# Hybrid attention and mLSTM layer on one core: two projections by seven products of quarter size in place of eight

## The chip, the core and the metric

The kernel runs on one core of a Trainium2 chip. The metric is the device time of one execution in microseconds; three runs of the kernel before have a median of 896.19 us (895.63 to 897.06). Engines are called PE (TensorE), DVE (VectorE), ACT (ScalarE), POOL (GpSimd) and SP (SyncE, which issues the transfers).

## What is computed

One decoder layer with two token mixers on the same normalised input of 512 tokens and 1024 channels. Cut to what matters:

```python
xn = rmsnorm(h, norm_in_g)
proj = xn @ w_in                                  # 1024 x 12288
q_a, k_a, v_a, z_a, x_m, z_m, o_m, gates = jnp.split(proj, SPLIT_POINTS, axis=-1)
y_a = (dilated_attention(q_a, k_a, v_a, rel_bias) * silu(z_a)) @ w_pa
y_m = mlstm_branch(x_m, z_m, o_m, ...) @ w_pb     # ends with  h * silu(z_m)
g = sigmoid(gates + gate_b)
g_a, g_m = jnp.split(g, 2, axis=-1)
h = h + (g_a * y_a + g_m * y_m) @ w_out
return rmsnorm(h, norm_out_g)
```

In the mLSTM branch x_m passes a causal convolution and a SiLU, gives q, k and v by small block-diagonal matrices, and each of four heads of 512 channels mixes the tokens with a decay from its input and forget gates; the result is gated with sigmoid(o_m), normalised, added to a skip of x_c, and multiplied with silu(z_m). z_m (2048 columns of w_in) and gates (2048 columns) are the two projections that the change touches.

## The kernel before

All data are float32, and each product is done in three: both factors are split into a high part (fp32r) and a low part, and `mm3` issues high x high, high x low and low x high into one PSUM bank. A projection takes w_in in 96 chunks of 1024 x 128 (on chip 128 x 1024: eight steps of 128 rows of the contraction). `weights` (L420) fetches a chunk on SP into a `raw` tile, and `halves` (L412) splits it: ACT copies it to `whi`, DVE subtracts to `wlo`. `proj_t` (L536) then makes 8 x 3 matmuls of 128 weight columns by 512 tokens into one of two banks of the tag "mm"; six other banks (tag "x") serve scores, transposes and the rest. There are four buffers each of `raw`, `whi` and `wlo`, and 51 "slot" tiles of 516 columns for everything of one token tile.

Stages, in order of the program: the x_m chunks with convolution, folded q/k and the score sums S of each head (`sraw`, four tiles that are kept in SBUF); the gate chain of the mLSTM (gsum, nab, ex, lnu, aa, aT); then for each head `head`(L777): decay weights Wh and Wl, num (60 matmuls), the gated and normalised tho, four z_m chunks with SiLU (`silu2`, L771), the transposes hT, then v and the output gate o_m of the next head (`block_v`, `gate_o`), and the ym projection; then attention (qa, ka, va, za, sa, pT, pv), the 16 gate chunks, ya, out and the last normalisation.

The order is not the program's. A `Recorder` (L101) collects every operation with its dependences, and `issue` (L231) simulates the five engines with a cost for each operation: when an engine is free, it issues the ready operation with the smallest priority for whose new tiles there is room. The priority is the place in the program less `R.ahead` (weights get `AHEAD` = 300, some evacuations of banks `EMPTY` = 300). The engines then run that order as it stands, each in order. All operations are recorded at one place, so the profile gives L333 as the line of every operation; the names of tiles tell them apart.

Of the kernel before, what the change touches and what calls it, by code (L numbers as in the profile page):

```python
# [11 lines left out]
F32 = mybir.dt.float32  # L12
F32R = mybir.dt.float32r
# [4 lines left out]
P = 128  # L18
# [319 lines left out]
def hybrid_layer(ctx, tc, a, out):  # L338
# [43 lines left out]
    def mm3(ps, lh, ll, rh, rl, first, last):  # L382
        PE.matmul(ps, lh, rh, start=first, stop=False)
        PE.matmul(ps, lh, rl, start=False, stop=False)
        PE.matmul(ps, ll, rh, start=False, stop=last)

    def rsqrt(v, n, name):
        y = small(name + "_y", n)
# [39 lines left out]

    ident = const("ident", [P, P], F32)
    pc = const("pc", [P, PC_N], F32)  # L430
    EARLY, UNNORMED, FIRST = 4, 10, 5
    pair = [wide("xt") for _ in range(NK // 2)]
# [5 lines left out]
    def x_split(k):  # L438
        h, l = slot("xh", F32R)[:, :T], slot("xl", F32R)[:, :T]
# [25 lines left out]
    xu = []  # L465
    early_ps = [mm_bank("xm") for _ in range(2)]
    for k in range(NK):
        xu.append(x_split(k))
# [54 lines left out]
        return m  # L523

    R.ahead = 5000
    early_m = [x_m(c, early_ps[c], rb) for c in range(EARLY)]
    R.ahead = 0
    xh, xl = [], []

    def normalise(k):  # L530
        V.tensor_mul(xt[k], xt[k], rb)
        h, l = x_split(k)
        xh.append(h)
        xl.append(l)
# [99 lines left out]
    sxd = dram("sxd", [NMT, P, T])  # L634
    v_of = {}

    def block_v(h):

        b = spread(brow[:, 2], h, "Bv")
        xm = []  # L640
        for c in range(4):
            x_ = slot("xmr")[:, :T]
            SP.dma_start(x_, xmd[4 * h + c])
            xm.append(x_)
        v_of[h] = []
        for s in range(NT):
            ps = sc_bank("v")
            for c in range(4):
                PE.matmul(ps[:, c * P:(c + 1) * P], xm[c][:, s * P:(s + 1) * P], b[:, c * P:(c + 1) * P],
                          start=True, stop=True)  # L650
            v1, v2 = slot("vh", F32R)[:, :514], slot("vl", F32R)[:, :514]
# [4 lines left out]
            v_of[h].append((v1, v2))  # L656

    gps = pv_bank("gates")
    sps = None
    waiting = []  # L660
    sraw = []
    for ct in range(NMT):
        h, c = divmod(ct, 4)
        raw_x = ct < UNNORMED
        ps = None if ct < EARLY else proj_t(CXM + ct, "xm", xu if raw_x else None)
# [21 lines left out]
        A.activation(kf, ps[:, T - P:], AF.Copy)  # L687
        if ct == 0:
            fold_gates()
        waiting.append((ct, m, xc))  # L690
        if c == 3:

            R.together()
            for ct_, m_, xc_ in waiting:
                for i, (w, x) in enumerate(((1, m_[:, 3:259]), (1, m_[:, 259:515]), (0, xc_[:, :256]), (0, xc_[:, 256:]))):
                    PE.matmul(gps[32 * i:32 * i + 32, :256], ust[w][:, ct_, :], x, start=ct_ == 0, stop=ct_ == NMT - 1,
                              tile_position=(0, 32 * i))
            R.apart()
            waiting = []
        for j in range(NT - 1):  # L700
            t0 = j * P
            ss = slice(t0, t0 + P)
            mm3(sps[j][:, :T - t0], kh[:, ss], kl[:, ss], ch[:, t0:], cl[:, t0:], c == 0, c == 3 and j < 2)
        PE.matmul(sps[2][:, 256:384], kf, xc[:, T - P:], start=False, stop=c == 3)
        if c == 3:
            sr = wide("sraw")
            A.activation(sr[:, 0:512], sps[0], AF.Copy)
            A.activation(sr[:, 512:896], sps[1][:, :384], AF.Copy)
            A.activation(sr[:, 896:1280], sps[2][:, :384], AF.Copy)
            sraw.append(sr)  # L710

    def row(name, dt=F32):
        return slot(name, dt)[:4, :T]
# [38 lines left out]
    selr = const("selr", [36, 4, P], F32)  # L752
    SP.dma_start(selr, a["sel"])
    sel = const("sel", [36, 4, P], F32R)
    V.tensor_copy(sel, selr)
# [18 lines left out]
        V.scalar_tensor_tensor(z, z, 1.0, ps, op0=OP.add, op1=OP.mult)  # L774
        return z

    def head(h):  # L777
        ps = sc_bank("Abc")
        PE.matmul(ps, sel[:, h, :], A2, start=True, stop=True)
        Abc = slot("Abc")[:, :T]  # L780
        A.activation(Abc, ps, AF.Copy)
        wh, wl = wide_t("Wh"), wide_t("Wl")
        sr = sraw[h]
        off = (0, 512, 896, 1152)
        for j in range(NT):
# [44 lines left out]
        V.tensor_mul(rs, rs, rr)  # L830
        for t in range(NT):
            V.tensor_scalar(us[t], us[t], mv[:, 2 * t:2 * t + 1], rs[:, t:t + 1], op0=OP.subtract, op1=OP.mult)
        z = [silu2(proj_t(CZM + 4 * h + c, "zm"), "zm") for c in range(4)]
        sx = []
        for c in range(4):
            x_ = slot("sxr")[:, :T]
# [32 lines left out]
    def rel_rows():  # L869
# [5 lines left out]
        G.tensor_copy(ohr, onehot)  # L875
# [17 lines left out]
    def values(p):  # L893
# [90 lines left out]


    ga = []
    for d in range(NK):
        for g in range(2):
            ps = proj_t(CG + NK * g + d, "gate")
            th = slot("thg")[:, :T]  # L990
            A.activation(th, ps, AF.Tanh, scale=0.5, bias=hs[:, 32 + 8 * g + d:33 + 8 * g + d])
            if g == 0:
                ga.append(th)
            else:
                V.scalar_tensor_tensor(ym[d], th, 1.0, ym[d], op0=OP.add, op1=OP.mult)
    go = const("go", [P, D], F32)
# [14 lines left out]
    for d in range(NK):  # L1011
        raw = raw_chunk("raw")
        SP.dma_start(raw, a["w_out"][d * P:(d + 1) * P, :])
        if d < 2:
            wl_ = wide("woh", F32R), wide("wol", F32R)
        elif d < 4:
            wl_ = wide_t("woh"), wide_t("wol")
        else:
            wl_ = None
        pieces = []  # L1020
# [39 lines left out]


NSMALL = 40
NSLOT = 51
NRAW = 4
NHL = 4
AHEAD = 300
EMPTY = 300
NWIDE = 4
NWT = 4


def _bucket(dist):
# [86 lines left out]
```

## Time and profile before

| | |
|---|---|
| median of 3 runs | 896.19 us |
| the profiled execution, its own time | 894.47 us |
| its span in the profile | 892.5 us |
| PE busy, matmuls | 879.0 us, 4340 |
| PE weight loads busy | 723.0 us |
| DVE busy | 573.9 us, 1193 instructions |
| ACT busy | 402.2 us, 750 instructions |
| moved by DMA | 104.64 MB, 117 GB/s on average |

The span is what the profiler sees from the first to the last instruction; the execution's own time is 1.97 us longer. On the scale of the span, the x_m stage ends at 157 us, head 0's om and the gate chain end at 177, the heads at 493, attention at 703, the gate chunks at 797, ya at 841, out at 886. A line of the profile names engine, operation, output and inputs (out<-in), and shapes. A matmul's listed duration contains pipelining, so that matmuls overlap; what one costs is the distance from one start to the next.

### The profile page before, as it was taken

How to read it: one execution, taken by the hardware profiler on the slowest of the kernel's cores; microseconds unless marked ns; L12 is line 12 of the kernel's file. 1: busy time of each engine (PE TensorE's matmuls, PEld its weight loads, DVE VectorE, ACT ScalarE, POOL GpSimd, SP SyncE). 2: the span in 40 equal slices, each digit the busy share in tenths (PEclk: the TensorE clock that was granted, in tenths of full speed). 3: DMA queues.
4: the chain of work that ended last, by engine and by line, in shares of the span. 5: the costliest groups of instructions: out<-in, count | busy, mean ns of one | idle time of the engine just before them, and what ended most of it. 6: DMA issues, size and time to landing. Idle time of an engine off the chain costs nothing.

```text
span 892.5 us, 11773 instructions
## 1 busy us (share of the span) xinstructions
PE 879.0 (98%) x4340; PEld 723.0 (81%) x4340; DVE 573.9 (64%) x1193; ACT 402.2 (45%) x750; POOL 11.2 (1%) x71
## 2 busy tenths in 40 slices
PE   7999999999999999999999999999999999999997
PEld 5778877788888888888888888888888888888886
DVE  4999997876256458735655477874787743338533
ACT  7435644713442323333232476755676633325222
POOL 0000000000000000000000000000000000000000
PEclk9999999999999999999999999999999999999999
DMA  9832533141258044125204223313222122225121
GB/s 301 303 131 87 186 116 142 52 161 48 103 197 303 23 151 157 71 95 175 73 25 145 104 83 107 105 49 118 84 95 84 59 95 95 94 95 167 69 89 53
DMA packets 38801, 104.64 MB, mean 117 GB/s; under 512 B 4308, under 2 KB 6100, under 8 KB 38744
## 3 DMA queue, kind: packets, MB, share of 16 engines
q1 hardware_dynamic: 38600, 103.63, 33.3%
q8 instruction: 34, 0.56, 0.2%
q10 hardware_dynamic: 144, 0.26, 0.1%
q14 instruction: 23, 0.19, 0.1%
HBM read 93.35 MB, written 15.77 MB: 122 GB/s over the span
## 4 chain that ended last, share of the span: by engine, by line
PE 93%; DMA 3%; DVE 1%; ACT 1%; SPq 0%; issue 0%; ACTq 0%; DVEq 0%
PE zm L333 10%; PE gate L333 10%; PE ym L333 10%; PE om L333 9%; PE xm L333 7%; PE out L333 5%; PE qa L333 5%; PE va L333 5%; PE ya L333 5%; PE ka L333 5%; PE za L333 5%; PE num L333 3%; PE S L333 3%; PE pv L333 2%; PE sa L333 2%; PE pT L333 2%
## 5 line engine op out<-in xcount | busy, mean ns | idle before, releaser
L333 DVE TENSOR_TENSOR wlo<-raw,whi 128x1024 fp32r<-128x1024 f32 (+1 forms) x126 | 147.4, 1173 | 156.1 <-ACT whi L333 156.1
L333 ACT ACTIVATE whi<-raw 128x1024 fp32r<-128x1024 f32 (+1 forms) x126 | 128.1, 1019 | 264.7 <-PE zm L333 74.8
L333 PE MATMUL xm<-xh,whi 128*128 128x512 f32 x128 | 52.0, 411 | 5.2 <-ACT whi L333 5.2
L333 PE MATMUL xm<-xh,wlo 128*128 128x512 f32 x128 | 51.3, 402 | 0.0
L333 PE MATMUL xm<-xl,whi 128*128 128x512 f32 x128 | 51.1, 401 | 0.0
L333 PE MATMUL gate<-xh,whi 128*128 128x512 f32 x128 | 50.8, 397 | 0.0
L333 PE MATMUL om<-whi,xl 128*128 128x512 f32 x128 | 50.8, 397 | 0.0
L333 PE MATMUL om<-whi,xh 128*128 128x512 f32 x128 | 50.8, 397 | 0.0
L333 PE MATMUL zm<-xh,whi 128*128 128x512 f32 x128 | 50.8, 397 | 0.0
L333 PE MATMUL om<-wlo,xh 128*128 128x512 f32 x128 | 50.7, 396 | 0.0
L333 PE MATMUL gate<-xh,wlo 128*128 128x512 f32 x128 | 50.7, 396 | 0.0
L333 PE MATMUL zm<-xh,wlo 128*128 128x512 f32 x128 | 50.5, 395 | 0.0
L333 PE MATMUL gate<-xl,whi 128*128 128x512 f32 x128 | 50.5, 395 | 0.0
L333 PE MATMUL ym<-yl,whi 128*128 128x512 f32 x128 | 50.5, 394 | 0.0
L333 PE MATMUL ym<-yh,whi 128*128 128x512 f32 x128 | 50.4, 394 | 0.0
L333 PE MATMUL ym<-yh,wlo 128*128 128x512 f32 x128 | 50.4, 394 | 0.0
L333 PE MATMUL zm<-xl,whi 128*128 128x512 f32 x128 | 50.2, 392 | 0.0
L333 ACT ACTIVATE p<-p,mx 128x128 f32<-128x128 f32 (+1 forms) x64 | 35.4, 556 | 14.6 <-DVE mx L333 14.6
L333 DVE CUSTOM_DVE_ANT_0 p<-sa,tb 128x128 f32<-128x128 f32 (+1 forms) x64 | 28.3, 486 | 18.2 <-PE sa L333 18.2
L333 DVE TENSOR_TENSOR ymacc<-ymacc,ym 128x512 f32<-128x512 f32 x24 | 16.5, 688 | 31.6 <-PE ym L333 31.6
L333 DVE SCALAR_TENSOR_TENSOR conv<-xm,half,conv 128x512 f32<-128x512 f32 x48 | 35.5, 744 | 0.3
L333 PEld LDWEIGHTS xm<-xh,whi 128*128 128x128 f32 x128 | 24.4, 192 | 10.9 <-ACT whi L333 5.5
(253 smaller groups left out, 2179.9 us busy)
## 6 DMA issues: line engine op xcount, KB each, us to landing
raw<-in_win_dram SPq DMA_DIRECT2D x94, 512.0 KB, 3.3
raw<-in_wpb_dram SPq DMA_DIRECT2D x16, 512.0 KB, 3.2
fr<-fd SPq DMA_DIRECT2D x1, 5120.0 KB, 22.4
xmd<-xm SPq DMA_DIRECT2D x16, 256.0 KB, 2.8
sxd<-sx SPq DMA_DIRECT2D x16, 256.0 KB, 2.0
xmr<-xmd SPq DMA_DIRECT2D x16, 256.0 KB, 4.8
sxr<-sxd SPq DMA_DIRECT2D x16, 256.0 KB, 4.2
tb<-fr SPq DMA_DIRECT2D x16, 256.0 KB, 3.7
```

The source lines that it names most:

```text
L333: getattr(getattr(self.nc, op.eng), fn)(*a, **k)
```

## The change

z_m and gates are computed in pairs of chunks, 16 pairs in all. Per pair, x (1024 channels x 512 tokens) and the two chunks are cut in quarters: the contraction in halves of four steps, the tokens in two halves of 256, the outputs in the two chunks. Seven products of quarters (a variant of Strassen's algorithm with shared sums) take the place of eight: 7 x 4 x 3 = 84 matmuls of 256 tokens for 2 x 8 x 3 = 48 of 512.

- `quarters`, once, after the twelfth of 16 x_m chunks: ACT scales x in place (8), DVE makes eight differences of 512 columns, ACT and DVE split them into `th` and `tl` (8 each).
- `pair_weights`, per pair: two chunks are fetched; four DVE operations of 512 columns make the weight sums (`s34` in two halves, `raw` in place, `s2`), which are split along with the chunks: three `halves` of 1024 columns and one of 512.
- `pair_t`, per pair: products into three banks, ba and bd of "mm" and bb of "x"; ACT copies two of them out, DVE combines with five operations of 256 columns. Four products are added to banks that ACT or DVE read in between (`skip_group_check`).
- `silu_pair` and the gate loop: tanh in two halves of 256 for the first chunk, whose result lies partly in a bank and partly in a slot.
- To make room: slots 51 to 44, `raw` 4 to 5, wide tiles 4 to 2 each, and a new tag "tx" of eight 128 x 1024 tiles (x, then parts of its split, then th and tl, then parts of w_out). `sraw` is stored to DRAM (640 KB a head) and loaded again in `head_weights`, which is split off `head` and runs for the next head ahead of `block_v`. `go` and `selr` become slot or wide tiles; onehot is converted on ACT, not POOL.
- `LEAD` = 1: an x_m chunk is projected one step ahead of its convolution.

```diff
+    def quarters():
+        for k in range(NK):
+            A.activation(xt[k], xt[k], AF.Copy, scale=gain(k))
...
+            V.tensor_sub(t[0], u[:, :, late], u[:, :, early])
+            V.tensor_sub(t[1], w[:, :, late], t[0])
+            V.tensor_sub(t[2], w[:, :, late], u[:, :, late])
+            V.tensor_sub(t[3], w[:, :, early], t[1])
...
+    def pair_weights(src0, src1):
...
+        s34, s2 = raw_chunk("s34"), tile_of(wpool, [P, 512], F32, "s2", "ws", NWS)
+        V.tensor_sub(s34[:, lo], r0[:, lo], r1[:, lo])
+        V.tensor_add(r1[:, lo], r1[:, lo], r1[:, hi])
+        V.tensor_sub(s2, r1[:, lo], r0[:, lo])
...
+        A.activation(h2, s2, AF.Copy)
+        V.tensor_sub(l2, s2, h2.bitcast(F32))
+        t0 = halves(r0)
+        t1 = halves(r1)
+        V.tensor_sub(s34[:, hi], r0[:, hi], s2)
+        t3 = halves(s34)
...
+    def pair_t(src0, src1, name):
+        w = pair_weights(src0, src1)
+        t1, t2, t3, t4 = tx
+        bb, ba, bd = sc_bank(name)[:, :256], mm_bank(name)[:, :256], mm_bank(name)[:, :256]
+        def product(ps, a, b, first):
+            kw = {} if first else {"skip_group_check": True}
+            for k in range(4):
+                cc = slice(k * P, k * P + P)
+                mm3(ps, a[0][:, cc], a[1][:, cc], b[k][0], b[k][1], first and k == 0, k == 3, **kw)
+        e, l = slice(0, 256), slice(256, 512)
+        p1, p6, c2 = slot("p1")[:, :512], slot("p6")[:, :512], slot("c2")[:, :512]
+        product(bb, w["s2"], t2, True)
+        R.ahead = EMPTY
+        A.activation(p6[:, e], bb, AF.Copy)
+        R.ahead = 0
+        product(ba, w["a11"], x_quarter(0, 0), True)
+        R.ahead = EMPTY
+        A.activation(p1[:, e], ba, AF.Copy)
+        R.ahead = 0
+        product(bd, w["s1"], t1, True)
+        R.ahead = EMPTY
+        V.tensor_add(p1[:, l], bd, p1[:, e])
+        R.ahead = 0
+        product(bb, w["s3"], t3, False)
+        R.ahead = EMPTY
+        V.tensor_add(c2[:, l], bb, p1[:, l])
+        R.ahead = 0
+        V.tensor_add(p6[:, e], p6[:, e], p1[:, e])
+        product(ba, w["a12"], x_quarter(1, 0), False)
+        product(bd, w["s4"], x_quarter(1, 1), False)
+        R.ahead = EMPTY
+        V.tensor_add(p6[:, l], bd, p6[:, e])
+        R.ahead = 0
+        product(bb, w["a22"], t4, False)
+        V.tensor_add(c2[:, e], bb, p1[:, e])
+        return (ba, p6[:, l]), c2
...
+            SP.dma_start(srd[h], sr)
+        if ct == 11:
+            R.ahead = -400
+            tx = quarters()
+            R.ahead = 0
...
-        sr = sraw[h]
+        sr = wide("sraw")
+        SP.dma_start(sr, srd[h])
...
-        z = [silu2(proj_t(CZM + 4 * h + c, "zm"), "zm") for c in range(4)]
+        for c in (0, 2):
+            z += silu_pair(a["win"][CZM + 4 * h + c], a["win"][CZM + 4 * h + c + 1], "zm")
...
-            ps = proj_t(CG + NK * g + d, "gate")
+            c1, c2 = pair_t(a["win"][CG + NK * g + d], a["win"][CG + NK * g + d + 1], "gate")
...
-NSLOT = 51
-NRAW = 4
+NSLOT = 44
+NRAW = 5
-NWIDE = 4
-NWT = 4
+NWIDE = 2
+NWT = 2
+NWS = 1
```

The planner makes a new order of all operations. Three places of it follow. The number behind a tile's name tells tiles of one name apart.

PE at the end of the last score sums S, where head 0's om follows; before:

```order
L333 MATMUL S_1471<-xch_1583,kph_1620 128x256
L333 MATMUL S_1471<-xcl_1603,kph_1620 128x256
L333 MATMUL S_1471<-xch_1583,kpl_1629 128x256
L333 MATMUL S_1471<-conv_1553,kf_1626 128x128
L333 MATMUL om_1531<-whi_1535,xl_1012 128x512
L333 MATMUL om_1656<-whi_1189,xh_775 128x512
L333 MATMUL om_1656<-wlo_1231,xh_775 128x512
```
and changed:

```order
L333 MATMUL S_1507<-xch_1661,kph_1696 128x256
L333 MATMUL S_1507<-xcl_1684,kph_1696 128x256
L333 MATMUL S_1507<-xch_1661,kpl_1701 128x256
L333 MATMUL S_1507<-conv_1614,kf_1699 128x128
L333 MATMUL om_1738<-whi_1214,xh_721 128x512
L333 MATMUL om_1738<-wlo_1241,xh_721 128x512
L333 MATMUL om_1738<-whi_1214,xl_743 128x512
```
Before, the last matmul of om_1531 and the start of om_1656 follow S; in the changed order it is a new group, om_1738. ACT in the same place, before:

```order
L333 ACTIVATE sraw_1641<-S_1459 128x512
L333 ACTIVATE sraw_1641<-S_1464 128x384
L333 ACTIVATE sraw_1641<-S_1471 128x384
L333 ACTIVATE tho_1659<-om_1531 128x512
L333 ACTIVATE ex_1663<-nab_1648 4x512
```
and changed:

```order
L333 ACTIVATE sraw_1713<-S_1492 128x512
L333 ACTIVATE sraw_1713<-S_1497 128x384
L333 ACTIVATE sraw_1713<-S_1507 128x384
L333 ACTIVATE ex_1725<-nab_1720 4x512
L333 ACTIVATE tho_1730<-om_1524 128x512
```
Before, tho takes om_1531 ahead of ex; in the changed order, ex comes first, and then tho, which reads om_1524, the group whose bank om_1738 takes.

DVE in the gate stage; before, with one split of weights (wlo) for 24 matmuls and the gated ym:

```order
L333 TENSOR_TENSOR yal_6794<-ya_4965,yah_5572 128x512
L333 TENSOR_TENSOR wlo_6808<-raw_6500,whi_6798 128x1024
L333 SCALAR_TENSOR_TENSOR ymacc_2332<-thg_6805,ymacc_2332 128x512
L333 TENSOR_TENSOR yal_6823<-ya_5238,yah_6812 128x512
L333 TENSOR_TENSOR wlo_6848<-raw_6562,whi_6838 128x1024
L333 TENSOR_TENSOR wlo_6881<-raw_6624,whi_6871 128x1024
L333 SCALAR_TENSOR_TENSOR ymacc_2351<-thg_6878,ymacc_2351 128x512
```
and changed, some of the stretch of one pair (s2, s34 and raw are weight sums, p1, p6 and c2 combinations of products):

```order
L333 TENSOR_TENSOR s2_7978<-raw_7837,raw_7813 128x512
L333 TENSOR_TENSOR p6_7952<-p6_7952,p1_7970 128x256
L333 TENSOR_TENSOR p1_7970<-gate_7965,p1_7970 128x256
L333 TENSOR_TENSOR s34_7940<-raw_7813,s2_7978 128x512
L333 TENSOR_TENSOR wlo_8003<-s2_7978,whi_7989 128x512
L333 TENSOR_TENSOR c2_8010<-gate_7928,p1_7970 128x256
L333 TENSOR_TENSOR wlo_8034<-raw_7813,whi_8021 128x1024
L333 TENSOR_TENSOR p6_7952<-gate_7965,p6_7952 128x256
L333 TENSOR_TENSOR wlo_8052<-raw_7837,whi_8039 128x1024
L333 TENSOR_TENSOR s34_8068<-raw_7943,raw_7967 128x512
L333 TENSOR_TENSOR wlo_8078<-s34_7940,whi_8060 128x1024
L333 TENSOR_TENSOR raw_7967<-raw_7967 128x512
```
The sums and splits of the next pair now lie between the combinations of the pair at hand.

PE in head 1, from the first products of the second z_m pair (zm_2936 is its bank bb, zm_2958 ba, zm_3022 bd):

```order
L333 MATMUL zm_2958<-xl_869,whi_2898 128x256
L333 MATMUL zm_2958<-xh_859,wlo_2923 128x256
L333 MATMUL hT_2980<-ident_101,tho_2391 128x128
L333 MATMUL hT_2982<-ident_101,tho_2391 128x128
...
L333 MATMUL zm_2958<-xl_1011,whi_2898 128x256
L333 MATMUL zm_2958<-xh_1005,wlo_2923 128x256
L333 MATMUL hT_2980<-ident_101,tho_2447 128x128
L333 MATMUL zm_3022<-th_1348,whi_2920 128x256
```
In the program the third product (bd) stands ahead of the fourth (bb) and fifth (ba); in this order it comes behind both and behind the first transposes hT.

## Rows read from the trace of the kernel before

**Rows 1.** The page, busy shares of the span, and busy tenths in 40 slices.
```profile
PE 879.0 (98%) x4340; PEld 723.0 (81%) x4340; DVE 573.9 (64%) x1193; ACT 402.2 (45%) x750; POOL 11.2 (1%) x71
...
PE   7999999999999999999999999999999999999997
...
DVE  4999997876256458735655477874787743338533
```

**Rows 2.** The page, the chain that ended last, share of the span by engine.
```profile
PE 93%; DMA 3%; DVE 1%; ACT 1%; SPq 0%; issue 0%; ACTq 0%; DVEq 0%
```

**Rows 3.** The chain in order of time (start, duration, what): head 0, head 1's num, gate.
```profile
177.34 7.14 PE num L333 x60
184.49 22.26 PE zm L333 x96
...
261.61 7.16 PE num L333 x60
...
715.97 80.86 PE gate L333 x349
```

**Rows 4.** Timeline of PE (start, duration, operation) near the end of the out stage.
```profile
883.74 0.28 PE L333 MATMUL out<-woh,mgh 128*128 128x256 f32 x1
...
885.76 0.28 PE L333 MATMUL out<-woh,mgl 128*128 128x256 f32 x1
```

**Rows 5.** Timeline of DVE in head 0, wide operations back to back.
```profile
207.89 1.22 DVE L333 TENSOR_TENSOR wlo<-raw,whi 128x1024 fp32r<-128x1024 f32 x1
209.02 0.68 DVE L333 SCALAR_TENSOR_TENSOR zm<-zm 128x512 f32<-128x512 f32 x1
209.62 0.68 DVE L333 TENSOR_TENSOR zm<-sxr,zm 128x512 f32<-128x512 f32 x1
```

**Rows 6.** Timeline of DVE in head 1's num stage, 256 columns.
```profile
264.62 0.38 DVE L333 SCALAR_TENSOR_TENSOR tho<-tho,num 128x256 f32<-128x256 f32 x1
264.93 0.14 DVE L333 TENSOR_SCALAR rr<-num 128x1 f32<-128x1 f32 x1
```

**Rows 7.** Windows: length; busy (count) of PE, PEld, DVE, ACT, POOL; PEclk, DMA share, GB/s.
```profile
42.00:157.00 115.00, 115.00 (x651) 91.89 (x651) 108.91 (x185) 55.71 (x104) 0.47 (x3) 1.00 0.37 134
177.00:257.00 80.00, 80.00 (x402) 66.82 (x400) 39.72 (x81) 26.97 (x39) 0.91 (x3) 1.00 0.31 110
716.00:797.00 81.00, 81.00 (x351) 65.62 (x350) 26.97 (x30) 26.97 (x36) 0.00 (x0) 1.00 0.26 93
```

**Rows 8.** Groups by line and form (busy us, mean ns), ACT, DVE and PE's weight loads.
```profile
L333 ACT ACTIVATE whi<-raw 128x1024 fp32r<-128x1024 f32 x118 | 125.1, 1060 | 264.5 <-PE zm L333 74.8 <-PE ym L333 57.8 <-PE gate L333 50.4
...
L333 DVE TENSOR_TENSOR wlo<-raw,whi 128x1024 fp32r<-128x1024 f32 x118 | 144.4, 1224 | 156.1 <-ACT whi L333 156.1
...
L333 PEld LDWEIGHTS num<-vh,Wh 128*128 128x128 f32 x80 | 15.2, 189 | 0.2
```

**Rows 9.** Timeline around the end of S at head 0.
```profile
157.25 1.42 ACT L333 ACTIVATE sraw<-S 128x512 f32<-128x512 f32 x3 [1.55 <-PE S L333]
...
157.76 0.67 DVE L333 SCALAR_TENSOR_TENSOR nab<-f 4x512 f32<-4x512 f32 x1
...
157.89 0.48 PE L333 MATMUL om<-whi,xl 128*128 128x512 f32 x1
...
158.56 0.59 ACT L333 ACTIVATE tho<-om 128x512 f32<-128x512 f32 x1
...
159.03 0.62 ACT L333 ACTIVATE ex<-nab 4x512 f32<-4x512 f32 x1
```

**Rows 10.** Timeline of DVE at the end of head 1's normalisation.
```profile
277.68 0.99 DVE L333 TENSOR_SCALAR tho<-tho,mv,rh_y 128x512 f32<-128x512 f32 x2
```

**Rows 11.** DMA issues from 255 to 295 us (KB each, median us to landing).
```profile
fr<-fd SPq DMA_DIRECT2D x1, 5120.0 KB, 22.4
...
xmr<-xmd SPq DMA_DIRECT2D x4, 256.0 KB, 14.8
sxr<-sxd SPq DMA_DIRECT2D x1, 256.0 KB, 16.8
```

More of the change, by code (lines that the diff above doesn't have):

```diff
@@ L380, in dram, with mm3 @@
         return R.buf(lambda: dpool.tile(shape, F32, name=name), shape, F32, dram=True)
[L382 to L385, printed above, removed]
+    def mm3(ps, lh, ll, rh, rl, first, last, **kw):
+        PE.matmul(ps, lh, rh, start=first, stop=False, **kw)
+        PE.matmul(ps, lh, rl, start=False, stop=False, **kw)
+        PE.matmul(ps, ll, rh, start=False, stop=last, **kw)
     def rsqrt(v, n, name):
@@ L430, in hybrid_layer @@
     pc = const("pc", [P, PC_N], F32)
-    EARLY, UNNORMED, FIRST = 4, 10, 5
-    pair = [wide("xt") for _ in range(NK // 2)]
+    EARLY, UNNORMED, FIRST, LEAD = 4, 10, 5, 1
+    pair = [tx_tile("xt", F32)[:, :] for _ in range(NK // 2)]
     xt = [pair[k // 2][:, k % 2 * T:k % 2 * T + T] for k in range(NK)]
@@ L525, in hybrid_layer @@
     R.ahead = 5000
-    early_m = [x_m(c, early_ps[c], rb) for c in range(EARLY)]
+    m_of = [x_m(c, early_ps[c], rb) for c in range(EARLY)]
     R.ahead = 0
@@ L534, in normalise @@
         xl.append(l)
+    def quarters():
+        for k in range(NK):
+            A.activation(xt[k], xt[k], AF.Copy, scale=gain(k))
+        x4 = [q.rearrange("p (k t) -> p k t", k=2) for q in pair]
+        early, late = slice(0, T // 2), slice(T // 2, T)
+        forms = []
+        for m in range(2):
+            u, w = x4[m], x4[m + 2]
+            t = [slot("tq")[:, :T].rearrange("p (k t) -> p k t", k=2) for _ in range(4)]
+            V.tensor_sub(t[0], u[:, :, late], u[:, :, early])
+            V.tensor_sub(t[1], w[:, :, late], t[0])
+            V.tensor_sub(t[2], w[:, :, late], u[:, :, late])
+            V.tensor_sub(t[3], w[:, :, early], t[1])
+            forms.append(t)
+        out = []
+        for i in range(4):
+            h, l = tx_tile("th"), tx_tile("tl")
+            for m in range(2):
+                cc = slice(m * T, m * T + T)
+                x = forms[m][i].rearrange("p k t -> p (k t)")
+                A.activation(h[:, cc], x, AF.Copy)
+                V.tensor_sub(l[:, cc], x, h[:, cc].bitcast(F32))
+            out.append([(h[:, k * 256:k * 256 + 256], l[:, k * 256:k * 256 + 256]) for k in range(NK // 2)])
+        return out
@@ new lines, in x_quarter @@
+    def x_quarter(r, c):
+        cc = slice(256 * c, 256 * c + 256)
+        return [(xh[k][:, cc], xl[k][:, cc]) for k in range(4 * r, 4 * r + 4)]
+    def pair_weights(src0, src1):
+        R.ahead = AHEAD
+        r0, r1 = fetch(src0), fetch(src1)
+        lo, hi = slice(0, 512), slice(512, 1024)
+        s34, s2 = raw_chunk("s34"), tile_of(wpool, [P, 512], F32, "s2", "ws", NWS)
+        V.tensor_sub(s34[:, lo], r0[:, lo], r1[:, lo])
+        V.tensor_add(r1[:, lo], r1[:, lo], r1[:, hi])
+        V.tensor_sub(s2, r1[:, lo], r0[:, lo])
+        h2 = tile_of(wpool, [P, 1024], F32R, "whi", "whi", NHL)[:, lo]
+        l2 = tile_of(wpool, [P, 1024], F32R, "wlo", "wlo", NHL)[:, lo]
+        A.activation(h2, s2, AF.Copy)
[5 more added lines that the diff above has]
+        R.ahead = 0
+        cut = lambda w, c: (w[0][:, c], w[1][:, c])
+        return dict(s2=(h2, l2), a11=cut(t0, lo), a12=cut(t0, hi), s1=cut(t1, lo), a22=cut(t1, hi),
+                    s3=cut(t3, lo), s4=cut(t3, hi))
@@ L536, in proj_t, with silu_pair @@
+    def silu_pair(src0, src1, name):
+        c1, c2 = pair_t(src0, src1, name)
+        z0 = slot(name)[:, :T]
+        for i in range(2):
+            h = z0[:, 256 * i:256 * i + 256]
+            A.activation(h, c1[i], AF.Tanh, scale=0.5)
+            V.scalar_tensor_tensor(h, h, 1.0, c1[i], op0=OP.add, op1=OP.mult)
+        return [z0, silu2(c2, name)]
     def proj_t(chunk, name, x=None):
@@ L660, in hybrid_layer @@
     waiting = []
-    sraw = []
     for ct in range(NMT):
         h, c = divmod(ct, 4)
-        raw_x = ct < UNNORMED
-        ps = None if ct < EARLY else proj_t(CXM + ct, "xm", xu if raw_x else None)
+        for e in range(max(EARLY, ct + LEAD) if ct else EARLY, min(ct + LEAD + 1, NMT)):
+            raw_x = e < UNNORMED
+            ps = proj_t(CXM + e, "xm", xu if raw_x else None)
+            R.ahead = EMPTY
+            m_of.append(x_m(e, ps, rb if raw_x else None))
+            R.ahead = 0
         if FIRST <= ct < FIRST + NK // 2:
@@ L709, in hybrid_layer @@
             A.activation(sr[:, 896:1280], sps[2][:, :384], AF.Copy)
-            sraw.append(sr)
+            SP.dma_start(srd[h], sr)
+        if ct == 11:
+            R.ahead = -400
+            tx = quarters()
+            R.ahead = 0
     def row(name, dt=F32):
@@ L775, in silu2, with head_weights @@
         return z
-    def head(h):
+    wt_of = {}
+    def head_weights(h):
         ps = sc_bank("Abc")
@@ L797, in head @@
             V.tensor_sub(wl[:, oo], e, wh[:, oo].bitcast(F32))
+        return wh, wl, off
+    def head(h):
+        wh, wl, off = wt_of.pop(h)
         vh, vl = zip(*v_of[h])
@@ L874, in rel_rows @@
         ohr, rel2 = wide("ohr", F32R)[:64, :640], const("rel2", [64, HEADS_A], F32R)
-        G.tensor_copy(ohr, onehot)
+        A.activation(ohr, onehot, AF.Copy)
         A.activation(rel2[:32], relb, AF.Copy)
@@ L1013, in hybrid_layer @@
         SP.dma_start(raw, a["w_out"][d * P:(d + 1) * P, :])
[L1014 to L1017, printed above, removed]
+        if d < 4:
+            wl_ = tx_tile("woh"), tx_tile("wol")
         else:
```

44 lines of the change are left out of this document (28 added, 16 removed).

## The prediction

> **What bounds the kernel now.** Start with the busy shares. PE is busy 879.0 of 892.5 us, and its row of tenths is 9 from the second slice to the last but one; DVE stands at 64% [rows 1]. Busy PE need not be the limit, so look at the chain of waits next: 93% of it is PE [rows 2], and in order of time it holds whole stages of PE without a gap, such as 96 zm matmuls in 22.26 us and 349 gate matmuls in 80.86 [rows 3]. So PE's count of matmuls sets the time, as long as ACT and DVE deliver weights and free banks in time. The 13.5 us in which PE is idle are mostly at the start and after the last matmul, where this change does nothing.
>
> **Terms on PE.** The 32 zm and gate chunks become 16 pairs. A pair had 2 x 8 x 3 = 48 matmuls of 512 columns; it gets 7 products x 4 x 3 = 84 of 256.
> - 512 columns: 80.86 / 349 = 0.2317 us each, with no gap between [rows 3].
> - 256 columns: the num stage, 256 and 258 columns, gives 7.14 / 60 = 0.119 [rows 3]; the out stage gives 2.02 us over 17 starts, 0.1188 [rows 4]. Both change the weights at each matmul, as the new ones do.
> - A pair: 48 x 0.2317 = 11.12 goes, 84 x 0.119 = 10.00 comes; 1.12 is saved, **18.0 us** over 16 pairs (177.9 out, 159.9 in). With 0.1188 it is 18.3; with the next num stage, 7.16 / 60 = 0.1193 [rows 3], it is 17.6.
>
> Removing an eighth of the arithmetic would give 22.2; the missing 4.2 lies in 0.119 being more than half of 0.2317. [...]
>
> **Terms on DVE and ACT.** DVE's new work for a pair is four sums of 512 (s34's two halves, the sum in place, s2), one split of 512, a third split of 1024 and five combinations of 256. Its cost is the distance between starts, since durations overlap: 1024 wide 209.02 - 207.89 = 1.13, 512 wide 0.60 [rows 5], 256 wide 264.93 - 264.62 = 0.31 [rows 6]. A gate pair then holds 5 x 0.60 + 3 x 1.13 + 5 x 0.31 and, averaged, one 512 sum for the gated ym (0.60): 8.54 us, against 10.00 of PE. [...] ACT gets 3.5 splits of 1.06 [rows 8], two 256 copies and the tanh, some 6 us a pair. So throughput suffices, with little slack on DVE, and I cost the sums and splits at nothing: what hides them is PE's 10.00 us. With summed durations, 1.22 for a split [rows 8], DVE would come to 9.9, about PE's own time; with two more 1024-wide operations, it would be the bound.
>
> There are four buffers of split weights, exactly one pair's. The buffer of the second product's weights is freed after the fifth product; the next pair needs it three products later, 3 x 12 x 0.119 = 4.28 us. The chain in between is a hand-over (about 0.2, as from om's end, 157.89 + 0.48 = 158.37, to tho at 158.56 [rows 9]), ACT 1.06, a hand-over, DVE 1.22 [rows 8] and a hand-over: 2.9. About 1.4 us is spare: one 1024-wide DVE operation in front fits, two don't.
>
> **xm stage.** It gets quarters(): 8 ACT copies of x and 8 splits' copies, 16 DVE subtractions of 512, plus the sums of the first pair: 20 x 0.60 = 12 us of DVE in a stretch where DVE works 108.91 of 115 [rows 7]. The order places 48 om matmuls ahead of S's end, where 22 stood: 26 x 0.2317 = 6.0 us of cover, and DVE's own 6.1 us of idle time is the other half. Bounds: 0 (all covered), 6.0 (none by the om work). I take 0, as PE has later work to bring forward at each place where DVE is late. The sraw stores (640 KB a head) and reloads take SP and DMA time at a DMA share of 0.31 to 0.37 [rows 7]; nothing, unless behind the transfer below. The conversion of onehot to ACT lies in the same slack.
>
> **Head 0's om, a new wait.** Before, after the last S matmul PE still has om's last matmul of one group and then the next group, whose bank is long free; tho is issued ahead of ex on ACT [rows 9]. In the changed order om_1738 stands right behind S, and takes the bank of om_1524; that bank is freed by tho_1730, which ACT issues after three sraw copies and after ex. ex waits for nab on DVE, and nab for the gate sums: 157.76 + 0.67 = 158.43. ex then runs 158.55 to 159.2 and tho 0.59 more, to 159.8; with a hand-over PE would start again near 160.0, against 157.89 [rows 9]. Queued behind the waiting om matmul is all of PE, so the **2.1 us** are lost whole. Bounds: 0 (tho gets done before S ends, if PE is late there) and 2.7 (one DVE operation of 0.60 [rows 5] ahead of nab).
>
> **Heads.** In each second zm pair the product s1 needs the bank of the first pair's c1, freed by DVE's silu sum; the order puts s3 and the fifth product ahead (24 x 0.119 = 2.9 us), which covers most. hT waits for the normalised tho, whose chain on DVE runs from num's end, 261.61 + 7.16 = 268.77 [rows 3], to 277.68 + 0.99 = 278.67 now [rows 10], and will hold new sums and splits in its gaps. Nearest row: DVE is busy 39.72 of 80 us in a head [rows 7], so a delay is one or two foreign operations. Bounds 0 and one 1.13 split for each of four heads, 4.5; I take a third, **+1.5**.
>
> The 5,120 KB transfer fr takes 22.4 us to landing, and those issued behind it 14.8 and 16.8, in the second stage of heads [rows 11]. In the new order a weight chunk of om, the sxr tiles and the raws of head 1's second pair go behind it. ACT and DVE, in order, hold the combinations of that pair while they wait for these raws. With 7.1 us of num and 10 of the first pair as cover, between 0 and 4 is left; I take **+1.0**.
>
> **Sum.** -18.0 + 2.1 + 1.5 + 1.0 = -13.4. Against the profiled execution, 894.47 us (span 892.5 and 1.97 around it), that makes 881.1. This execution lies 1.7 under the median of the runs, 896.19; from the median it is 882.8. I forecast **882.5**.
>
> **Rivals.**
> - *The waits are filled by the order.* PE takes other matmuls at each place; the 18.0 arrives whole, 878.2. For it: PE's row shows almost no wait now although all its feeders wait on it. Against: ACT and DVE are in order, and the tho place is visible in the order.
> - *DVE in front, in part.* In the gate and zm pairs two DVE operations stand ahead of a split: 0.6 us a pair (2 x 1.13 - 1.4 = 0.9 at two of three buffers). 16 x 0.6 = 9.6 less of the 18: with head 0's 2.1, 889.9. For it: 85% on one in-order engine that also waits for ACT.
> - *The four split buffers decide; slower.* The next pair's split is issued on ACT behind copies of products that PE has not made, and the buffer is used late each time. It breaks even at (18.0 - 2.1) / 16 = 1.0 us a pair; one whole round of ACT and DVE, 1.06 + 1.22, less the spare, a combination 0.31 and its hand-overs 0.4 give 1.6 us a pair, 26 us; the time is 896.2 - 18.0 + 26 + 2.1 = 906. Against: the order already interleaves next pair's splits with this one's combinations, as the DVE rows of the change show.
> - *Weight loads serialise.* The trace has loads of 189 ns at a distance of 119: 60 of them are 11.3 us inside num's 7.14 [rows 3, 8], so they overlap with matmuls. If they did not, a pair would take 84 x 0.189 = 15.9, 4.8 more than now, 76 in all: 972. [...]
>
> That the change doesn't do what it says is excluded by the order: 84 matmuls of 256 stand for each pair.
>
> **How the numbers follow.** The forecast gets 0.62, the full saving 0.12, DVE in front 0.18, the split buffers 0.07, serial loads 0.01. The forecast's own bounds run from 878 (waits 0) to 890 (17.6 saved, 2.7 + 4.5 + 4 lost); with the full saving's 878.2 in it, the range is 877.5 to 890; outside lie the slower rivals and half of DVE in front. No change means within 0.2%, 1.8 us, about what a measurement of this kernel can tell. Faster 0.90; between, a stall of near 1.0 us a pair, 0.03; slower 0.07.
>
> **What would show it.** Right: zm and gate matmuls of 256, 84 a pair at 0.119; one PE gap of about 2 us at head 0's om, released by ACT's tho; DVE's share near 76% (573.9 and some 100 of new work over 881), near 85% in the gate stage, and that stage 9 us shorter. A gate matmul that waits for DVE's wlo or ACT's whi, again at each pair, would make the second or third rival true. Matmuls of zm at over 0.12 without a wait would break the first term itself.

## The result, and the profile after

The changed kernel takes **891.28 us** (median of 5 runs, 889.5 to 892.05), the kernel before in the same comparison 895.63: a ratio of 0.9947, 95% interval [0.9932, 0.9961]. It is faster, by 4.4 us, where 13.7 were forecast; the time lies above the range of 877.5 to 890. The profiled execution took 889.50 us, with a span of 887.7.

The page of the changed kernel, shares of the span and the chain that ended last:

```profile
PE 865.2 (97%) x4916; PEld 741.2 (83%) x4916; DVE 674.9 (76%) x1393; ACT 452.0 (51%) x847; POOL 11.0 (1%) x70
...
PE   7999999899999899999999999999999999999997
...
PE 82%; DVE 9%; DMA 4%; ACT 3%; issue 2%; SPq 0%; ACTq 0%; DVEq 0%
```

Against [rows 1, 2]: 576 more matmuls, and yet 13.8 us less of busy PE; but PE's idle time went from 13.5 to 22.5 us, two slices of its row are now 8, and the chain is 82% PE where it was 93%. So PE got its saving, and something now waits. The chain in order of time shows the saving, and the windows the stage that the prediction feared most:

```profile
429.35 19.97 PE zm L333 x168
...
731.09 60.75 PE gate L333 x511
```

```profile
707.00:792.00 85.00, 85.00 (x708) 84.59 (x707) 77.47 (x147) 56.96 (x102) 0.35 (x2) 1.00 0.35 109
42.00:161.00 119.00, 116.19 (x629) 93.60 (x628) 116.73 (x202) 64.05 (x117) 0.77 (x5) 1.00 0.41 140
```

(columns as in [rows 7].) Both stretches run at 19.97 / 168 = 60.75 / 511 = 0.1189 us a matmul. The gate stage keeps PE busy for 85.00 of 85 us although DVE is at 77.47, 91%; on the chain it lasts from 707.35 to 791.84, 84.5 us, against 702.59 to 796.83 before, though 14 of its 672 matmuls now stand ahead of it. What is lost is lost earlier: in the xm stage PE works 116.19 of 119 us, where it worked all of 115 [rows 7]. The list of PE's waits names the places (total, times, longest):

```profile
PE xm L333 <- ACT whi L333: 5.5, 2, 5.2
PE zm L333 <- DVE p L333: 3.5, 1, 3.5
PE om L333 <- ACT tho L333: 1.7, 1, 1.7
PE om L333 <- ACT xm L333: 1.1, 1, 1.1
PE v L333 <- DMA xmr<-xmd: 0.8, 1, 0.8
PE xm L333 <- ACT xh L333: 0.7, 1, 0.7
PE S L333 <- ACT kph L333: 0.6, 2, 0.3
...
PE xm L333 <- DVE xl L333: 0.4, 1, 0.4
```

The first is the start of the program, as before. The third is the wait that the prediction foresaw. The second is the largest behind it, in head 1. The chain from 255 to 300 us tells where it comes from:

```profile
262.61 3.38 DMA fd<-frow
265.99 0.02 issue
266.00 0.61 SPq L333
266.62 0.05 issue
266.67 22.53 DMA raw<-in_win_dram
...
289.30 1.07 ACT whi L333
290.37 0.02 issue
290.39 1.23 DVE wlo L333
291.62 0.34 DVE p L333
291.96 0.04 issue
292.00 4.37 PE zm L333 x24
```

SP issues fr at 266.00 (5,120 KB, 22.0 us to landing, so at 288.0), and a weight chunk of om right behind it, which lands after 22.53 us, at 289.2. ACT's and DVE's rows in that stretch:

```profile
284.50 0.63 ACT L333 ACTIVATE zm<-c 128x512 f32<-128x512 f32 x1 [2.07 <-DVE c L333]
289.30 1.06 ACT L333 ACTIVATE whi<-raw 128x1024 fp32r<-128x1024 f32 x1 [4.17 <-DMA raw<-in_win_dram]
290.26 0.37 ACT L333 ACTIVATE zm<-zm 128x256 f32<-128x256 f32 x1
```

```profile
290.39 1.23 DVE L333 TENSOR_TENSOR wlo<-raw,whi 128x1024 fp32r<-128x1024 f32 x1 [4.39 <-ACT whi L333]
291.53 0.42 DVE L333 TENSOR_TENSOR p<-zm,p 128x256 f32<-128x256 f32 x1
```

ACT stands in front of the split of that chunk, and DVE in front of the same chunk's wlo. PE has no use for the chunk yet: 24 matmuls of z_m are still to come before the next om. Behind the wlo on DVE stands p, a combination of 0.42 us that frees a bank of the pair that PE is working on. PE waits for that:

```profile
292.00 0.58 PE L333 MATMUL zm<-xh,whi 128*128 128x256 f32 x1 [3.54 <-DVE p L333]
292.38 0.42 PE L333 MATMUL zm<-xl,whi 128*128 128x256 f32 x1
292.60 0.42 PE L333 MATMUL zm<-xh,wlo 128*128 128x256 f32 x1
...
294.91 0.28 PE L333 MATMUL zm<-tl,whi 128*128 128x256 f32 x1
295.03 0.28 PE L333 MATMUL zm<-th,wlo 128*128 128x256 f32 x1
```

and the clock granted to PE falls for the next stretch, from 1.00 to 0.50:

```profile
288.20:291.40 3.20, 0.27 (x1) 0.00 (x0) 1.01 (x1) 1.33 (x2) 0.00 (x0) 1.00 0.85 303
291.50:294.70 3.20, 2.69 (x12) 2.70 (x13) 3.03 (x7) 0.00 (x0) 0.00 (x0) 0.50 0.94 352
295.00:300.00 5.00, 5.00 (x29) 4.28 (x28) 4.75 (x8) 4.29 (x7) 0.00 (x0) 1.00 0.46 176
```

12 matmuls are about 0.215 us apart instead of 0.119, which adds 12 x 0.096 = 1.15 to the wait.

To count losses too small for a list of waits, each matmul's distance to the next start was taken less the median distance for its shape (0.232 for 512 columns, 0.118 for 256), and summed by stage. This **excess** is worked out from all PE rows of a trace. Kernels e6, e9 and e10 are those of the experiments below.

| excess, us | before | changed | e6 | e9 | e10 |
|---|---|---|---|---|---|
| to the end of S | 12.7 | 16.0 | 15.6 | 14.7 | 12.9 |
| gate chain, first om, to num | 1.3 | 3.5 | 3.5 | 2.7 | 0.9 |
| head 0 | -0.1 | 1.5 | 1.6 | 1.2 | 2.3 |
| head 1 | 0.0 | 5.6 | 1.9 | 1.9 | 2.0 |
| heads 2 and 3 | 0.9 | 0.8 | 0.2 | 0.7 | 0.8 |
| attention, to the last pv | 0.4 | 1.8 | 1.9 | 1.1 | 1.5 |
| gate, ya, out | -0.2 | 0.6 | 0.5 | 0.3 | 0.3 |
| sum | 15.0 | 29.8 | 25.2 | 22.6 | 20.7 |
| span less the sum | 877.5 | 857.9 | 857.9 | 857.9 | 857.9 |

The last row is the same for the four kernels with the change: back to back, PE's work is 19.6 us shorter, of which about 1.2 returns as excess, since the 1344 new matmuls stand 0.1189 apart and not 0.118. The excess rose by 14.8, and so of the 19.6 only 4.8 is left, the difference of the two spans.

The profiled execution is 1.8 us under the median of the five. Its mean granted clock is 0.997; the other four runs have 0.994 or 0.995. Estimated from these, 0.002 to 0.003 of 888 us is 1.8 to 2.7 us, so more time at the lower clock could account for the difference. It isn't shown, as their traces aren't at hand. In the kernels without the wait in head 1 (e1, e6) the clock is 0.998 or 0.999 in all runs, and the profiled execution is not under the median by more than 0.1 us.

### The profile page after: what moved, and what is told of

It is laid out like the page before. It is cut to its first block, busy times and chain, and to the rows that moved or that the text cites. A ratio compares the mean times of both kernels' runs of the same rounds, so it can differ in the third digit from the quotient of the medians.

```text
span 887.7 us, 13352 instructions
## 1 busy us (share of the span) xinstructions
PE 865.2 (97%) x4916; PEld 741.2 (83%) x4916; DVE 674.9 (76%) x1393; ACT 452.0 (51%) x847; POOL 11.0 (1%) x70
## 4 chain that ended last, share of the span: by engine, by line
PE 82%; DVE 9%; DMA 4%; ACT 3%; issue 2%; SPq 0%; ACTq 0%; DVEq 0%
PE ym L333 10%; PE gate L333 9%; PE om L333 9%; PE zm L333 6%; PE xm L333 6%; PE ya L333 5%; PE out L333 5%; PE va L333 5%; PE qa L333 5%; PE za L333 5%; PE ka L333 4%; DMA raw<-in_win_dram 3%; DVE conv L333 3%; PE num L333 2%; PE sa L333 2%; PE pv L333 2%
## 5 line engine op out<-in xcount | busy, mean ns | idle before, releaser
L333 ACT ACTIVATE whi<-s 128x512 fp32r<-128x512 f32 (+1 forms) x32 | 26.9, 842 | 49.4 <-PE ym L333 11.9
L333 PE MATMUL zm<-th,whi 128*128 128x256 f32 x128 | 36.4, 284 | 0.0
L333 PE MATMUL gate<-th,wlo 128*128 128x256 f32 x128 | 36.3, 284 | 0.0
L333 PE MATMUL gate<-tl,whi 128*128 128x256 f32 x128 | 36.2, 283 | 0.0
L333 PE MATMUL zm<-th,wlo 128*128 128x256 f32 x128 | 36.1, 282 | 0.0
L333 PE MATMUL zm<-tl,whi 128*128 128x256 f32 x128 | 36.1, 282 | 0.0
L333 PE MATMUL gate<-th,whi 128*128 128x256 f32 x128 | 35.9, 282 | 0.0
L333 PE MATMUL xm<-xh,whi 128*128 128x512 f32 x88 | 34.8, 397 | 0.7 <-ACT xh L333 0.7
L333 PE MATMUL xm<-xl,whi 128*128 128x512 f32 x88 | 35.0, 398 | 0.4 <-DVE xl L333 0.4
L333 PE MATMUL xm<-xh,wlo 128*128 128x512 f32 x88 | 35.0, 397 | 0.0
```

Source lines behind the costliest of these rows:

```text
L333: getattr(getattr(self.nc, op.eng), fn)(*a, **k)
```

## The experiments

Each ratio is to the kernel before, run on the same chip; the changed kernel stands at 0.9947. A profile shows one execution, and the changed kernel's is 1.8 us under its median; so what an experiment gains by the ratios can be more than its profile shows.

**e1: fr on another queue.** PE, DVE and ACT keep the changed kernel's order row for row.

```diff
-        SP.dma_start(fr, fd[:, None, :].to_broadcast([16, P, 640]))
+        G.dma_start(fr, fd[:, None, :].to_broadcast([16, P, 640]))
```

> The changed kernel with one edit: the 5,120 KB transfer fr is issued on POOL's queue; PE, DVE and ACT keep their order row for row. Theory: the om weights wait behind fr in SP's queue (22.5 us to landing), ACT and DVE hold the combinations of head 1's second z_m pair behind them, PE waits 3.5 us and then runs 12 matmuls at the lower clock (0.215 against 0.119 us): 3.8 + 1.15 = 4.9 us go, 891.3 becomes about 886.4, and that chunk lands in under 8 us. Rival: it is bandwidth, not the queue's order; then the chunk still lands after 15 us or more, a gap of 2 us or more stays at head 1, and the time is 889 to 891.

886.83 us, ratio 0.9895 [0.9873, 0.9917]. The wait of z_m for p is gone, and what was behind fr lands earlier (issues from 255 to 300 us):

```profile
fr<-fd POOLq DMA_DIRECT2D x1, 5120.0 KB, 28.2
raw<-in_win_dram SPq DMA_DIRECT2D x5, 512.0 KB, 8.9
...
sxr<-sxd SPq DMA_DIRECT2D x4, 256.0 KB, 10.4
```

The chunk that took 22.53 us now lands after 5.0; it starts at 266.43, 0.24 us ahead of fr. The four sxr loads start within 1.6 us behind fr and land 12 us or more ahead of it. So the place in the queue made the wait, as the theory has it. The time fell by about what was forecast, 4.7 us by the ratios for 4.9, but the profiled executions differ by 2.2 only: head 1's excess falls from 5.6 to about 2.6, not to nothing. The rival has a share: while fr runs, the core's DMA moves about 340 GB/s (mean of the slices from 267 to 294 us), hardly more than the 325 of the changed kernel from 266 to 288; fr takes 28.2 us for 22.0, two chunks that start at 279.5 and 280.9 take 12.7 and 13.3, and in head 1 v waits 1.2 us for xmr.

**e2: fr in 16 pieces on SP,** in the program one after each bn_stats of heads 1 to 3 and four more in head 3. The planner did not leave them there: in the trace twelve pieces are issued from 266.3 to 278.3 us and four from 295.6 to 297.4, all in head 1, with other loads between them.

```diff
-        SP.dma_start(fr, fd[:, None, :].to_broadcast([16, P, 640]))
+        SP.dma_start(fr[r], fd[r:r + 1].to_broadcast([P, 640]))
```

> The changed kernel with fr written in 16 pieces of 320 KB, spread over heads 1 to 3 on SP; the planner makes a new order. Theory as in e1: no transfer holds SP's queue for more than about 2 us, no PE gap of over 1 us in heads 1 to 3, about 886 to 887. Rival (the stall has another cause, the pair's combinations behind splits): a gap of 2 us or more remains at some second z_m pair of heads 1 to 3, 889 or more.

887.88 us, ratio 0.9907 [0.9886, 0.9928]. The wait of z_m is gone. Of v's waits for xmr (2.7 us in three places) the longest, 1.5, is in head 0, ahead of fr; head 1 has 0.4 and 0.8, and heads 1 to 3 have no gap of over 1 us. The theory held, but the time is about 1 us above its window. What it shows is the effect of many small transfers in place of one, not of spreading them over three heads.

**e3: 46 slots for 44** (`NSLOT = 46`; a new order of all engines).

> The changed kernel with 46 slots in place of 44; the planner makes a new order, in which tho stands ahead of ex on ACT. Theory: tho of head 0, whose om group ends at 150 us, waits for a free slot until 168 us; with two more, PE's 1.9 us at the first om matmul after S go, and 891.3 becomes about 889.4. Rival: the gate chain (nab, ex) holds ACT there whatever the slots; the gap stays at 1.5 us or more, and so does the time, 890.5 to 892.

886.61 us, ratio 0.9893 [0.9869, 0.9917]. The time fell by more than forecast, but not for the reason given. Though tho is now ahead of ex on ACT, the wait for it went only from 1.7 to 1.1 us: the three sraw copies still stand in front. The excess fell by 3.0 us, in several places (1.4 to the end of S, 0.8 in the gate chain, 0.5 in attention): the shortage of slots costs a little in many. The rest of the 4.8 us that the ratios show lies in runs without a profile. The wait at fr is as before:

```profile
PE zm L333 <- DVE p L333: 3.6, 1, 3.6
```

**e4: without the work of quarters** (z_m and gates are then other sums).

```diff
-            tx = quarters()
+            tx = [x_quarter(i // 2, i % 2) for i in range(4)]
```

> The changed kernel without the work of quarters: the four forms of x are taken to be quarters of the split x, so 16 DVE and 16 ACT operations of 512 columns are left out (z_m and gates are then other sums). Theory: these operations are what PE's further waits in the x_m stage come from (excess over back-to-back matmuls up to the end of S 16.0 us, 12.7 before the change); without them it is about 12.7 to 13.5 and the time 3 us less, about 888. Rival: the shortage of slots and the earlier projection (LEAD) cause them; the excess falls by less than 1 us, the time is 890 to 891.

886.33 us, ratio 0.9888 [0.9866, 0.9910], a fall of 5.3 us where 3 were forecast. The excess to the end of S falls from 16.0 to 12.7, and in the gate chain from 3.5 to 1.5; the wait of om for tho is gone from the list. So the 16 DVE and 16 ACT operations of quarters, with the order that they bring, cost 3.3 us in the xm stage, and the first om's wait hangs on them as well: without them 24 om matmuls stand ahead of S's end, not 48, and other om work is left behind S. That 12.7 is also the excess of before is in part chance: xm's waits for xh and xl stay in e4 (0.7 and 0.4 us), and before has 1.2 for kp that e4 lacks. The wait at fr stays (4.2 us).

What quarters do to PE can be read in the changed kernel. ACT copies xm out of its bank behind three copies of quarters (th), and om waits for that bank:

```profile
142.07 1.67 ACT L333 ACTIVATE th<-tq 128x512 fp32r<-128x512 f32 x3
143.63 0.59 ACT L333 ACTIVATE xm<-xm 128x512 f32<-128x512 f32 x1
```

```profile
144.28 0.50 PE L333 MATMUL om<-whi,xh 128*128 128x512 f32 x1 [1.10 <-ACT xm L333]
```

**e5: e1 and e3 together.**

> The changed kernel with fr on POOL's queue (as e1) and 46 slots (as e3). Theory: the two losses are apart (head 1; x_m stage and first om), so the gains add: from 891.3, 4.5 for e1 and about 4.7 for e3 less what e3 got outside of its place, 882 to 883. Rival: e3's gain lay in where its new order put heads and attention, or in runs with a milder stall at fr; then e5 is within 1.5 us of e1, 885.5 to 887.

886.95 us, 884.14 to 890.17, ratio 0.9909 [0.9877, 0.9940]. The rival won: no more than either alone. With fr on its own queue and this order, PE waits for transfers once more (v for xmr 3.0 in two places, one of them 2.1 in head 1, om for wlo 0.8), the granted clock is 0.50 from 302.5 to 305.7 us, after that one (16 matmuls of v take 3.40 us to the next start, where 16 of them take 1.70 in the changed kernel from 382.19 us), and head 1's excess is 6.2. The profiled execution is 1.9 us above this median. A separate queue does not make fr's 5,120 KB free, and where its cost falls depends on the order.

**e6: the planner is told the rate.** fr stays on SP's queue.

```diff
-                    link = begin + max(math.prod(shape) * 4 / 359, 64)
+                    link = begin + max(math.prod(shape) * 4 / (234 if math.prod(shape) > 1 << 20 else 359), 64)
```

> The changed kernel, fr on SP's queue as in the change, but the planner is told the rate that fr has on the chip: transfers of over 4 MB at 234 bytes per ns in place of 359 (5,120 KB in 22.4 us, 14.6 us by the planner's own rate). Theory: the change's order puts the om weights behind fr because the planner believes that they land 8 us earlier; told the rate, it moves other work in between, and PE's gap in head 1 falls below 1 us, time 886 to 888. Rival: the order cannot avoid it with fr at that place; the gap of 3 us or more stays, 890 or more.

885.05 us (884.66 to 885.44), ratio 0.9886 [0.9870, 0.9903]. SP's order around fr is that of the changed kernel, but ACT's isn't:

```profile
284.13 0.63 ACT L333 ACTIVATE zm<-c 128x512 f32<-128x512 f32 x1 [2.08 <-DVE c L333]
284.73 0.38 ACT L333 ACTIVATE zm<-zm 128x256 f32<-128x256 f32 x1
289.05 0.42 ACT L333 ACTIVATE zm<-p 128x256 f32<-128x256 f32 x1 [3.94 <-DVE p L333]
290.54 0.63 ACT L333 ACTIVATE zm<-c 128x512 f32<-128x512 f32 x1 [1.07 <-DVE c L333]
291.07 0.58 ACT L333 ACTIVATE Abc<-Abc 128x512 f32<-128x512 f32 x1
291.55 1.05 ACT L333 ACTIVATE whi<-raw 128x1024 fp32r<-128x1024 f32 x1
```

The split of the late chunk now stands behind the pair's own work. The chunk lands as late as ever, after 22.8 us, and nobody waits: in the list of PE's waits no z_m is left. This settles the cause of head 1's loss: a cost in the planner that is 8 us short for one transfer put an operation that waits for it in front of operations that PE needs.

**e7: only the gates by seven products** (e5, with z_m's four `silu2(proj_t(...))` of before put back).

> e5 with z_m computed as before (eight products, 512 columns), so only the gate chunks go by seven products. Theory: z_m's eight pairs are worth their 8 x 1.12 = 9.0 us of PE and cost no waits of their own in the heads, so this is 9 us above e5, 891 to 892. Rival: the sums of z_m in the heads cost waits that eat half of it; then it is at most 5 us above e5.

888.13 us, ratio 0.9920 [0.9906, 0.9935]: only 1.2 us above e5, where the theory had 9, so the rival won; and 4.9 above e9. The excess in the four heads is 0.9, as before the change. So in e5 the z_m half, worth 9.0 us on PE by the prediction's terms, gave some 7.8 back in waits, and in e9 some 4.1; e5's runs spread over 6 us, and e9 has another queue for fr and another rate, so these are rough. The gate half came through nearly whole. Though its queue and slots differ, this kernel with half of the change beats the whole change as it was made.

**e8: the kernel before with fr on POOL's queue,** a control for e1.

> The kernel before with fr on POOL's queue; PE, DVE and ACT keep their order. Theory: nothing waited for fr before (all PE gaps of heads 1 to 3 together 0.3 us), so no change: 896.5 within 1 us. Rival: the queue is worth something in itself, 2 us or more faster, and e1's gain is not the change's loss.

894.44 us against 895.55, ratio 0.9991 [0.9975, 1.0006]. No difference outside the interval; e1's gain is the undoing of a loss that the change brought.

**e9: e6 and e3 together** (rate told, 46 slots).

> The changed kernel with fr on SP's queue, the planner told the rate of large transfers (as e6), and 46 slots (as e3). Theory: e6 left excess of 5.1 us in the x_m stage and the first om above that of before, and e3 took about 2 us off it and 0.5 off attention, so this is 2 to 3 us under e6, 882 to 883. Rival: as in e5, the new order meets the transfers behind fr at another place (xmr, om's weights), and the gain in the x_m stage is given back there; 885 to 887.

**883.19 us** (882.38 to 883.57), ratio 0.9865 [0.9848, 0.9881]. This beats both kernels, 12.3 us under that of before, and is close to the time that was forecast for the change, though by a path with two causes of waits taken out. PE's waits that are left:

```profile
PE om L333 <- DVE wlo L333: 1.1, 1, 1.1
PE om L333 <- ACT tho L333: 1.1, 1, 1.1
PE kp L333 <- ACT xch L333: 0.8, 1, 0.8
```

**e10: e9 without the work of quarters** (edit as in e4; again other sums).

> e9 without the work of quarters (as e4: the forms of x are quarters of the split x, z_m and gates are other sums). Theory: with the x_m stage, the first om and fr all undone, what is left of the change is 18 us of PE less about 3 for the waits on xmr in the heads and 1 in attention: excess over back-to-back about 17 to 19 us (before 15.0), time 878 to 880. Rival: the saving on PE itself is smaller than 18; then the excess is as low, but the time is 883 or more.

880.97 us, ratio 0.9839 [0.9824, 0.9854]: 1 us above the window that was given, with the excess at 20.7 and not 17 to 19. The rival is out, since span less excess is 857.9 here too: PE's saving is what the rows said. The rest is in head 0 (v for xmr, 1.4), head 1 (om for wlo, 1.0) and attention. What quarters cost in e9's order is thus about 883.19 - 880.97 = 2.2 us.

**e11: less lead for weights** (e9 with `AHEAD = 200`).

> e9 with the lead of weights over other work in the planner's priorities 200 places in place of 300. Theory: what remains in the heads is waits on transfers behind fr and on DVE's splits in front of combinations; with less lead, fewer chunks stand ahead of them, 1 to 2 us under e9. Rival: weights then come late in the pairs, each pair needing its four buffers at once; gaps in front of z_m and gate matmuls, and slower than e9.

883.82 us, ratio 0.9874 [0.9853, 0.9895]: no difference to e9. Two waits of om for wlo stand in head 1 in place of one; no matmul of z_m or gate waits. Neither prediction came true, and the lead of the weights is not what is left.

**e12: fr after head 2** (e9 with `if h == 2:` ahead of `rel_rows`).

> e9 with fr made after head 2 in place of head 0, so that it is moved in the last head, which loads no xmr for a next head. Theory: the 1.9 us of excess that e9 has left in head 1 is what is queued behind fr (om's weights: a wait of 1.25 for wlo); it goes, and the last head, which has va in place of v and om, covers fr: 881 to 882. Rival: head 1's wait is DVE's own (splits and combinations in one row), it stays, and fr costs its wait in the last head as well: 883 to 885.

884.99 us, ratio 0.9873 [0.9848, 0.9898], which is not clear of e9's by the intervals. Head 1's excess falls from 1.9 to 0.2, so it was fr's, as the theory had it and against the rival. But heads 2 and 3 have 2.8 in place of 0.7, with the same wait of PE for wlo, now at va (0.6): as the rival had it, fr costs its wait where it is put. The profiled execution also lost 2 us more ahead of the heads, most of it in one wait of kp (2.7 for 0.8), and that can't be put down to fr.

## Why the prediction was wrong, step by step

The step that failed is what PE's saving gives back in waits. The saving came as forecast. But fr's term, +1.0 us, measured 5.6: a load queued behind fr held ACT and DVE in front of a combination that frees PE's bank. And the xm stage, put at nothing, cost 3.3. The time of 891.3 is near that of the rival with DVE in front (890), but that is chance: the waits it counts on don't occur.

- **PE, 18.0 us: right.** 0.119 was forecast for a matmul, 0.1189 measured, in both stages; span less excess is 19.6 us shorter, and about 18.4 with the distance of the new matmuls. Weight loads overlap: in the gate stage 707 of them are busy for 84.59 us beside 85.00 of matmuls, so the rival of serial loads (972) is out.
- **DVE and ACT in the gate stage, nothing: right,** though DVE is at 91%, not 85%: PE doesn't wait once for a split or a combination. The turn-over of the four split buffers never shows. Both rivals built on it (890 and 906) are out. (The 9.9 us a pair for summed durations is 9.65 by the rows shown; nothing hangs on it.)
- **Head 0's om, 2.1 us: right.** 1.7 of wait, 1.9 of excess, released by tho; the whole gate chain and first om have 2.2 more than before. With tho ahead of ex (e3) 1.1 of the 1.7 stays, behind the three sraw copies. What was not seen is that quarters cause this too (e4).
- **xm stage, 0 of 0 to 6.0: failed.** It cost 3.3 us. The sum put 6.0 of new om work against the 12 us of DVE work as if cover could be moved to where it is needed. (The trace has 23 om matmuls ahead of S's end before, not 22, so it is 25 x 0.2317 = 5.8.) But the waits of PE's list that go with quarters (e4) are for single operations, xm's copy (1.1 us) and kph (0.6). Both are released by ACT, which works in order, and xm's copy stood behind ACT's own part of quarters; om matmuls stood elsewhere. The sum looked at DVE's room, 108.91 of 115 [rows 7], and gave ACT's copies no place in an order. What DVE's part of the 3.3 is, e4 can't tell, as it takes out both.
- **Heads, +1.5: size right by luck, mechanism wrong.** Neither s1's bank nor hT made PE wait. In head 0, which has 1.6 more, the one gap is v for xmr, 0.8 of wait and 1.0 of excess: SP issues these loads at 211.3 to 215.5 us, behind four of w_pb, where before it issued them at 176 to 182. Why they come so late is not shown.
- **fr, +1.0 of 0 to 4: the step that failed most.** The place and the mechanism were named much as they happened: loads behind fr, ACT and DVE in order in front of the combinations of head 1's second pair. Only the chunk was another, one that PE needs later. But the excess of head 1 is 5.6, 3.8 of it the gap and 1.2 the slower matmuls behind it. The bound of 4 did not follow from the prediction's own numbers: fr's 22.4 and the split behind it, 1.06 + 1.22, less the 17.1 of num and the first pair, are 7.6. And nothing in the sum stood for the clock.
- **Attention, +1.4, and the profiled run's offset, 1.8:** neither was in the sum. Slots have a part in the first (e3 0.5 less).

The sum was -18.0 + 4.6. By the table it is -19.6 (distances of 0.118) + 3.3 (xm stage) + 2.2 (gate chain) + 1.6 (head 0) + 5.6 (head 1) + 1.4 (attention) + 0.7 (the rest) = -4.8, the difference of the two spans.

What stays open: the clock's part in the runs that were not profiled (e5's runs of 884.14 and 890.17 us have the same mean clock, 0.996, so it is not the whole of the spread), why xmr comes late in head 0, and what in attention waits longer.

## What to carry to other kernels

Where engines run a fixed order made by a cost model, look for the operation whose real cost is furthest from the model's, above all a large transfer, and see what stands behind it in each in-order queue: the largest loss here came from one transfer that was 8 us slower than the planner believed, and one number in the planner brought over 5 us back (0.9947 to 0.9886). Work added to engines that run in order was not covered here by other work on PE: in the xm stage quarters cost 3.3 us, though 5.8 us of om work stood there to cover them. So ask for each matmul which single operation it waits for, and what stands in front of that in its engine's order, ACT's no less than the busiest engine's. A saving that needs buffers pays for them: two slots more brought 2 us (e9 against e6) or more (e3).

## What the runs showed of the hardware

In the changed kernel nothing that is issued on the same queue behind the 5,120 KB transfer lands before it, in all of its 22.0 us: the chunk that is issued 0.67 us behind it takes 22.53 us to land, against a median of 3.7 in the whole run, and the four sxr loads, issued 8.8 to 14.0 us behind it, take 11.8 to 15.0, against 5.1. With fr on POOL's queue (e1) the four sxr loads behind it land after 7.5 to 14.1 us, well ahead of it, though fr slows from 22.0 to 28.2 us.

After the gap of 3.5 us in head 1 the granted clock was 0.50 from 291.5 to 294.7 us, and 1.00 again from 295 us, so the wait cost 1.15 us on top of itself. e3 and e4 have the same wait (3.6 and 4.2 us); the mean granted clock of their profiled executions is 0.996 and 0.995, against 0.997 in the changed kernel, and 0.998, 0.998 and 0.997 in e1, e6 and e9, which don't have it.
